# The last 256 output columns of the expert down-projection, made 128 at a time, and the final sums of squares moved from GpSimd to TensorE

## The chip, the cores and the metric

The kernel runs on one core of a Trainium2 chip. The metric is the device time of one execution in microseconds. Of the kernel before there are three timed executions, from 1497.66 to 1500.59 us with a median of 1499.51 us, and one profiled execution of 1500.35 us.

## The reference

The reference computes one layer of a decoder for 288 tokens (256 of a prompt, 8 times 4 of a sample batch) with 2048 channels. The part that matters here is its end: a mixture of 32 experts (gated MLPs with 512 hidden channels each), and after it a gated per-layer embedding and a last normalization. With `h` the residual stream, the end is

```
h = h + sum over the chosen experts e of  weight[e] * (act[e] @ w_down[e])      # 512 -> 2048 for each expert
u = rmsnorm(h, g_ple)                                                             # over the 2048 channels
h = h + sigmoid(u @ w_ple_gate + b_ple_gate) * (p @ w_ple_proj)                   # 2048 -> 2048
y = rmsnorm(h, g_final)
```

`w_down` has 32 x 512 x 2048 fp32 numbers (134 MB), `w_ple_gate` 2048 x 2048 (16.8 MB). Each channel of the second matrix product needs all 2048 channels of `h`, and each norm needs the sum of squares of all of them.

## The kernel before

Everything lies with channels on partitions: `hT` is 16 rows (c = 0 to 15) of 128 channels by 288 tokens. The stage around the change begins when the experts' hidden activations are ready.

The down-projection (the loop that ends the function, L1419 to L1446) runs over 8 blocks of 256 output columns, that is two rows of `hT` each. In a block it runs over 10 units of experts, in the order W N N W N W N W N N: a unit W is two experts with 64 token slots each, a unit N four experts with 32 slots each. A pair of experts is one transfer (L1428) of 128 x 2048 numbers, 1 MB, issued from SyncE's queue into half of a 2 MB slot of the pool `ws1`. There are four slots; a slot is taken again (`wtile`) when the matmuls on its old content are done. For each unit `down` (L1110) makes `Y`, tokens by columns, in PSUM (L1114), and ScalarE and VectorE split it into a high and a low half (`Yh` L1118, `Yl` L1119). One unit later `turn_` (L1410) calls `back`, which multiplies by the unit's 0/1 matrix so that the result stands by channels and tokens (`yp`, L1129, two rows by two matmuls) and adds it to `hT` (L1131, VectorE).

In the same loop the second product is worked off for the rows that are already finished. When block m has begun, the two rows of block m - 1 are final (`final`, L1353) and 16 "gates" are queued, one for each output row c of `z`: `ev_z` (L1403) multiplies the two finished rows by their part of `w_ple_gate` with three matmuls for each row (`mm3`, L229 to L231: high x high, low x high, high x low) and VectorE adds the result to `z` (L1408). `turn_` runs one gate behind a unit W and two behind a unit N. The gate weights come in transfers of 512 KB (`w_pg`, L1371) into `wraw`, which has two buffers. `halves` splits them into `whi` (ScalarE, L225) and `wlo` (VectorE, L226), two buffers each. All these transfers stand in SyncE's queue in program order, so a transfer that waits for a buffer holds up those behind it.

The gates for the last two rows (14 and 15) can't run until the last weights are used. Their weights are loaded at the end by `last_halves` (L1384 to L1400): two transfers into `wraw` (L1392), and one of 1 MB into a weight slot (L1395).

The end (L1519 to L1598) is written out by hand for TensorE, ScalarE and VectorE. `start_z` (L1476) brings a row of `z` into PSUM by a product with the identity, and `gate` adds the six matmuls of rows 14 and 15. VectorE multiplies by the inverse norm (`mul`, L1487), ScalarE takes the sigmoid (L1488), VectorE multiplies by the projected embedding (`f2a`, L1492) and adds to `hT` (`f2b`, L1495), ScalarE squares (`f3`, L1498). The squares are summed over the rows by GpSimd for rows 0 to 11 (`f4p`, L1504 and L1507), and over the channels by TensorE (`f4`, `token_sums` L1464, three matmuls with one column each). `warm(n)` (L1460) is n matmuls whose result nobody reads. Then the inverse root (L253 to L258), `spread` (L290), which brings it to all partitions, the last product (L1596) and the transfers out (L1597).

Of the kernel before, what the change touches and what calls it, by code (L numbers as in the profile page):

```python
# [20 lines left out]
D = 2048  # L21
# [95 lines left out]
def hymba_kernel(ctx, tc, a):  # L117
# [990 lines left out]
    def down(c0, nd, at, sc, ws, wt, two=None):  # L1108
# [7 lines left out]
        if two:  # L1116
            Yh, Yl = (two.tile([128, nd * 128], F32R, name=nm, bufs=2) for nm in ("Yh", "Yl"))
# [222 lines left out]
    last = KD // 2 - 1  # L1340

# [11 lines left out]
    def final(m):  # L1353

        gparts(m)
        for k in range(2):
            c = 2 * m + k
# [8 lines left out]
    def ready(g):  # L1366

        for i in range(max(wg, default=-1) + 1, min(g + 2, 8 * last)):
# [7 lines left out]
    def gate(m, acc, hi, lo, first=True):  # L1376

        gh, gl = gp[m]
        for k in range(2):
            mm3(acc, hi[:, k, :], lo[:, k, :], gh[:, k, :], gl[:, k, :], first and k == 0, k == 1)  # L1380
# [4 lines left out]
    def last_halves(eng=None):  # L1385
# [3 lines left out]
        if i % 2 == 0:  # L1389
            if i < 4:  # L1390
                wr[0] = tl.tile([128, 8, 128], F32, name="wraw", bufs=2)
                dma(wr[0].rearrange("p k c -> p (k c)"), a["w_pg"][28 + i // 2])  # L1392
            elif i == 4:
                t = wtile()[:, 0]
                dma(t.rearrange("p (r a) b -> p r (a b)", r=2), a["w_pg"][30:32].rearrange("r p x -> p r x"))  # L1395
                wr[1] = t.rearrange("p a (k c) -> p (a k) c", c=128)
        src = wr[0][:, 4 * (i % 2):4 * (i % 2) + 4, :] if i < 4 else wr[1][:, 4 * (i % 4):4 * (i % 4) + 4, :]
        hi, lo = (x[:, 4 * (i % 4):4 * (i % 4) + 4, :] for x in pw[i // 4 * 2:i // 4 * 2 + 2])
        nc.scalar.copy(hi, src)
        (eng or nc.vector).tensor_sub(lo, src, hi.bitcast(F32))  # L1400

    def ev_z(m, c):
        acc = psA([128, NTOK], "acc")  # L1403
        gate(m, acc, *[x[:, 2 * (c % 2):2 * (c % 2) + 2, :] for x in ready(8 * m + c // 2)])
# [10 lines left out]

    with tc.manual_schedule(engines={mybir.EngineType.PE}):
        gates += [lambda: None] * 2
        for m in range(KD // 2):
            for u, (s0, ne) in enumerate(units):  # L1419
                wt = []  # L1420
                for i in range(s0 // 2, (s0 + ne) // 2):
                    if not half:
                        t = wtile()
                        half += [t[:, 0], t[:, 1]]
                    t = half.pop(0)
                    src = a["w_down"][m]
                    src = src[0] if i == 0 else src[pair_of(i)].rearrange("o p x -> (o p) x")
                    dma(t, src.rearrange("p (a b) -> p a b", a=4))  # L1428
                    v = t.rearrange("p (e a) (b c) -> p e (a b) c", e=2, c=256)
# [3 lines left out]
                if u == 0 and m:  # L1433
                    final(m - 1)
                    gates += [lambda c=c, m=m: ev_z(m - 1, c) for c in range(KD)]
                back.append(b)
                if m == last:
                    if u == 4:
                        pw.append(ws1.tile([128, 16, 128], F32R, name=pslots[0]))
                    if u == 8:  # L1440
                        t = ws1.tile([128, 2, 16, 128], F32R, name=slots.pop(0)[1])
                        pw += [t[:, 0], None, t[:, 1]]
                        last_halves()
                        last_halves()
# [25 lines left out]
    sqs = tl.tile([128, NTOK], F32, name="sqs")  # L1470
# [29 lines left out]
    def f4p(c):  # L1500

        x = sqt[:, c % 4:c % 4 + 2, :]
        if c == 0:
            nc.gpsimd.tensor_add(sqs, x[:, 0, :], x[:, 1, :])  # L1504
        else:
            for i in range(2):
                nc.gpsimd.tensor_add(sqs, sqs, x[:, i, :])  # L1507

    def f4(c):
        token_sums(pf, sqt[:, c % 4, :], c == 12, c == KD - 1)  # L1510
# [4 lines left out]
    c0 = KD - 2  # L1515
    with tc.manual_schedule(engines={E.PE, E.Activation, E.DVE}):
# [10 lines left out]
        last_halves(nc.gpsimd)  # L1527
        last_halves(nc.gpsimd)
        nc.scalar.activation(gh[:, 0, :], hT[:, c0, :], AF.Copy, scale=prm("g_ple", c0))
        nc.vector.tensor_mul(sqt[:, 0, :], hT[:, c0, :], hT[:, c0, :])  # L1530
        nc.scalar.activation(sqt[:, 1, :], hT[:, c0 + 1, :], AF.Square)
        nc.vector.scalar_tensor_tensor(gl[:, 0, :], hT[:, c0, :], prm("g_ple", c0), gh[:, 0, :].bitcast(F32),
                                       op0=ALU.mult, op1=ALU.subtract)
        split(gh[:, 1, :], gl[:, 1, :], hT[:, c0 + 1, :], prm("g_ple", c0 + 1))
        for c in range(1, 3):
            start_z(c)
        for i in range(2):
            token_sums(ssp, sqt[:, i, :], False, i == 1)
# [6 lines left out]
        last_halves(nc.gpsimd)  # L1545
# [6 lines left out]
        for p in range(KD // 2):  # L1552
# [9 lines left out]
            if nh[0] < 8:  # L1562
                last_halves(nc.gpsimd)
            f0(c + 6)
            f0(c + 7)
            if p > 1:
                if c - 4 < 12:
                    f4p(c - 4)
                else:
                    f4(c - 4)  # L1570
# [119 lines left out]
```

## Time and profile before

| | |
|---|---|
| timed, median of 3 | 1499.51 us (1497.66 to 1500.59) |
| profiled execution | 1500.35 us, span 1498.7 us |
| mean granted TensorE clock | 0.947 |
| TensorE busy | 1300.5 us (87%) |
| VectorE / ScalarE / GpSimd busy | 553.5 / 392.0 / 23.1 us |
| DMA | 518.32 MB, mean 346 GB/s |

The span runs from the first instruction to the last. The profiled execution took 1.65 us more than its span. The down-projection's first weights are used at about 1096 us, its last at 1451 us; what comes after that, to 1498.7 us, is called the tail below.

### The profile page before, as it was taken

To read this page: it belongs to the slowest core of one execution; us is meant where nothing else is said; L and a number is where in the kernel's file an instruction comes from. 1 tells how busy PE (TensorE), PEld (TensorE's weight loads), DVE (VectorE), ACT (ScalarE), POOL (GpSimd) and SP (SyncE) were. 2 spreads that over 40 slices of the span, in tenths; PEclk is the share of its full clock that TensorE was granted. 3 is DMA by queue.
4 is the path that set the end of the run, shared out by engine and by line. 5 is a ranking of instruction groups with operands and counts; after the bars stand their busy time and mean duration, and the time that the engine had idled before them with its cause. 6 is when DMAs were issued, how large, how long until landed. Compare 5 with 4: busy or idle time off the path is not lost.

```text
span 1498.7 us, 24037 instructions
## 1 busy us (share of the span) xinstructions
PE 1300.5 (87%) x9535; PEld 851.1 (57%) x9535; DVE 553.5 (37%) x1322; ACT 392.0 (26%) x744; POOL 23.1 (2%) x26
## 2 busy tenths in 40 slices
PE   7999888799999988775978868869778999999996
PEld 7997677588996444222523423416235666666675
DVE  6765545666663100000000000003023455555557
ACT  6535434655441100000000000002013322222335
POOL 0000000000000000000000000000000000000014
PEclk9999998999999999987999989979899999999997
DMA  7879787532776899999999999999999999999971
GB/s 271 275 242 295 240 277 246 160 141 76 266 273 266 352 396 427 428 427 428 417 428 427 428 428 427 427 426 426 393 418 419 419 419 419 419 419 418 420 287 64
DMA packets 80841, 518.32 MB, mean 346 GB/s; under 512 B 10705, under 2 KB 12818, under 8 KB 47826
## 3 DMA queue, kind: packets, MB, share of 16 engines
q1 hardware_dynamic: 80066, 514.33, 86.3%
q0 software_dynamic: 656, 2.39, 0.4%
q8 instruction: 77, 1.26, 0.3%
q14 instruction: 42, 0.34, 0.1%
HBM read 513.81 MB, written 2.88 MB: 345 GB/s over the span
## 4 chain that ended last, share of the span: by engine, by line
DMA 35%; PE 15%; DVE 2%; issue 1%; ACT 0%; DVEq 0%; SPq 0%; ACTq 0%
DMA w<-in_w_down 21%; DMA w<-in_w_up 8%; PE Gp L1081 6%; DMA w<-in_w_gate 5%; PE xp L1054 4%; PE Y L1114 2%; PE pp L1280 1%; DMA wpp<-in_w_pp 1%; DVE gtt L1492 1%; DVE hT L1495 0%; DVE gtt L1487 0%; DVE hT L1596 0%; PE yp L1129 0%; PE s L1464 0%; PE acc L1460 0%
## 5 line engine op out<-in xcount | busy, mean ns | idle before, releaser
L1081 PE MATMUL Gp<-w,Xq 128*32 128x512 f32 (+1 forms) x2048 | 356.8, 673 | 93.4 <-DMA w<-in_w_up 50.1
L1081 PEld LDWEIGHTS Gp<-w,Xq 128*32 128x32 f32 (+1 forms) x2048 | 89.7, 127 | 318.7 <-issue 175.9
L229 PE MATMUL acc<-uh,whi 128*128 128x288 f32 x496 | 155.6, 314 | 14.9 <-ACT whi L219 7.4
L231 PE MATMUL acc<-uh,wlo 128*128 128x288 f32 x496 | 153.8, 310 | 3.5 <-DVE wlo L220 3.4
L230 PE MATMUL acc<-ul,whi 128*128 128x288 f32 x496 | 152.4, 307 | 0.4 <-DVE ul L264 0.4
L1090 DVE SCALAR_TENSOR_TENSOR Yb<-Gp,rs,Yb 128x512 f32<-128x512 f32 x10 | 7.5, 751 | 341.8 <-PE Gp L1081 307.5
L1131 DVE TENSOR_TENSOR hT<-hT,yp 128x288 f32<-128x288 f32 x160 | 71.2, 450 | 165.2 <-PE yp L1129 165.2
L1054 PE MATMUL xp<-Pq,hn 96*128 96x256 f32 (+1 forms) x576 | 119.8, 360 | 12.8 <-issue 12.0
L1114 PE MATMUL Y<-w,w 128*32 128x256 f32 (+1 forms) x1280 | 113.8, 389 | 19.2 <-DMA w<-in_w_down 19.1
L1054 PEld LDWEIGHTS xp<-Pq,hn 96*128 96x128 f32 x576 | 97.2, 197 | 53.9 <-issue 42.6
L229 PEld LDWEIGHTS acc<-uh,whi 128*128 128x128 f32 x496 | 97.9, 197 | 19.0 <-ACT whi L219 9.2
L220 DVE TENSOR_TENSOR wlo<-wraw,whi 128x1024 fp32r<-128x1024 f32 x82 | 99.9, 1220 | 18.6 <-PE acc L231 9.8
L231 PEld LDWEIGHTS acc<-uh,wlo 128*128 128x128 f32 x496 | 98.0, 198 | 7.4 <-DVE wlo L220 5.8
L219 ACT CAST whi<-wraw 128x1024 fp32r<-128x1024 f32 x82 | 85.4, 1042 | 63.9 <-PE acc L230 45.5
L230 PEld LDWEIGHTS acc<-ul,whi 128*128 128x128 f32 x496 | 98.2, 198 | 1.6 <-DVE ul L264 0.9
L1114 PEld LDWEIGHTS Y<-w,w 128*32 128x32 f32 (+1 forms) x1280 | 51.7, 116 | 66.2 <-DMA w<-in_w_down 34.1
L1058 DVE TENSOR_SCALAR Xq<-xp,P 128x256 f32<-128x256 f32 (+1 forms) x48 | 21.1, 440 | 168.5 <-PE xp L1054 168.5
L1118 ACT ACTIVATE Yh<-Y,wsl 128x256 fp32r<-128x256 f32 x80 | 37.9, 473 | 173.6 <-PE Y L1114 172.9
L1089 ACT ACTIVATE Yb<-Gp,rs 128x512 f32<-128x512 f32 x10 | 6.9, 687 | 283.9 <-PE Gp L1081 278.4
L1114 PE MATMUL Y<-w,wl 128*32 128x256 f32 (+1 forms) x768 | 72.3, 389 | 8.9 <-DMA w<-in_w_down 8.9
L1056 ACT ACTIVATE Xq<-xp,P 128x256 f32<-128x256 f32 (+1 forms) x48 | 21.0, 438 | 189.8 <-PE xp L1054 189.8
L231 PE MATMUL acc<-gh,wlo 128*128 128x288 f32 x224 | 66.1, 295 | 1.3 <-DVE wlo L226 1.3
(487 smaller groups left out, 1868.8 us busy)
## 6 DMA issues: line engine op xcount, KB each, us to landing
w<-in_w_gate SPq DMA_DIRECT2D x64, 2048.0 KB, 26.0
w<-in_w_up SPq DMA_DIRECT2D x64, 2048.0 KB, 24.8
w<-in_w_down SPq DMA_DIRECT2D x128, 1024.0 KB, 17.1
kv<-in_cache SPq DMA_DIRECT2D x128, 288.0 KB, 3.9
wraw<-in_w_in SPq DMA_DIRECT2D x44, 512.0 KB, 4.8
wraw<-in_w_o SPq DMA_DIRECT2D x32, 512.0 KB, 4.0
wraw<-in_w_pg SPq DMA_DIRECT2D x30, 512.0 KB, 15.2
wraw<-in_w_uq SPq DMA_DIRECT2D x6, 512.0 KB, 4.1
```

Of the source, the lines that this page charges most:

```text
L219: nc.scalar.copy(hi[:, x, :], r[:, x, :])
L220: nc.vector.tensor_sub(lo[:, x, :], r[:, x, :], hi[:, x, :].bitcast(F32))
L229: nc.tensor.matmul(out, hi, xh, start=start, stop=False)
L230: nc.tensor.matmul(out, hi, xl, start=False, stop=False)
L231: nc.tensor.matmul(out, lo, xh, start=False, stop=stop)
L1054: nc.tensor.matmul(xp, hn[:, t, d * 128:(d + 1) * 128], Pq[:, t, :n], start=t == 0, stop=t == 2)
L1056: nc.scalar.activation(X[:, d, :n], xp, AF.Copy, scale=prm("g_ffn", d))
L1058: nc.vector.tensor_scalar(X[:, d, :n], xp, prm("g_ffn", d), None, op0=ALU.mult)
L1081: nc.tensor.matmul(acts[j][sl * e:sl * e + sl, :], X[:, kk, o:o + sl], wt[e](k), start=kk == 0, stop=kk == KD - 1)
L1114: nc.tensor.matmul(Y[sl * e:sl * e + sl, :], at[:, f, sl * e:sl * e + sl], w(f), start=f == 0, stop=f == 3)
L1118: nc.scalar.activation(Yh, Y, AF.Copy, scale=ws)
L1131: nc.vector.tensor_add(h_, h_, yp)
```

## The change

The eight blocks of 256 columns become seven of 256 and two of 128. `w_down` is passed as two arrays, `w_down2` with seven blocks and `w_down1` with two; in the last two blocks a pair is a transfer of 512 KB, four to a slot (`wpart`). A block of 128 columns has one row of `hT`, so its `Y` has 128 columns and `back` one `yp` of two matmuls.

When the first of the two narrow blocks is done, row 14 is final. Its 16 gates, of three matmuls each instead of six, are worked off in the last block; `ready` now loads `w_pg` for it too (L1371 becomes L1382). Only row 15 is left for the tail. Its weights, two transfers of 512 KB, are loaded inside the last block by `last_halves` behind units 5 and 7 and split there by ScalarE and VectorE, into a slot taken out of the weights' four at unit 4. In the tail the gate of a row of `z` is three matmuls instead of six, and GpSimd has nothing to do: `f4p` is gone, and `f4` on TensorE sums the squares of all 16 rows. `warm(3)` becomes `warm(2)`.

```diff
+    blocks = [*((2 * m, 2) for m in range(7)), (14, 1), (15, 1)]
+    rows_ = [(2 * m, 2) for m in range(KD // 2 - 1)] + [(KD - 2, 1), (KD - 1, 1)]
+    last = len(rows_) - 1
...
-        for i in range(max(wg, default=-1) + 1, min(g + 2, 8 * last)):
+        for i in range(max(wg, default=-1) + 1, min(g + 2, 60)):
...
     def gate(m, acc, hi, lo, first=True):
         gh, gl = gp[m]
-        for k in range(2):
-            mm3(acc, hi[:, k, :], lo[:, k, :], gh[:, k, :], gl[:, k, :], first and k == 0, k == 1)
+        n = rows_[m][1]
+        for k in range(n):
+            mm3(acc, hi[:, k, :], lo[:, k, :], gh[:, k, :], gl[:, k, :], first and k == 0, k == n - 1)
...
+    def last_halves():
         i = nh[0]
         nh[0] += 1
         if i % 2 == 0:
...
+            wr[1] = tl.tile([128, 8, 128], F32, name="wraw", bufs=2)
+            dma(wr[1].rearrange("p k c -> p (k c)"), a["w_pg"][30 + i // 2])
+        halves(*(x[:, 4 * i:4 * i + 4, :] for x in pw), wr[1][:, 4 * (i % 2):4 * (i % 2) + 4, :])
...
+    def wpart(n):
+        if n == 4:
+            return wtile().rearrange("p e f c -> p (e f c)")
+        if not half or half[0].shape[1] != 1024 * n:
+            t = wtile().rearrange("p e f c -> p (e f c)")
+            half[:] = [t[:, 1024 * n * i:1024 * n * (i + 1)] for i in range(4 // n)]
+        return half.pop(0)
...
-                b = down(2 * m, 2, at[u], sc[u], ws[:, u:u + 1], wt, tl)
-                turn_(ne // 2 + (m == last and u in (6, 8)))
+                b = down(c0, nd, at[u], sc[u], ws[:, u:u + 1], wt, tl)
+                turn_(ne // 2 * max(1, bd // 2))
...
+                if n == len(blocks) - 1:
                     if u == 4:
                         pw.append(ws1.tile([128, 16, 128], F32R, name=pslots[0]))
...
+                        pw.append(ws1.tile([128, 2, 16, 128], F32R, name=slots.pop(0)[1])[:, 0])
+                    if u in (5, 6, 7, 8):
                         last_halves()
...
     def f4(c):
-        token_sums(pf, sqt[:, c % 4, :], c == 12, c == KD - 1)
+        token_sums(pf, sqt[:, c % 4, :], c == 0, c == KD - 1)
...
-                if c - 4 < 12:
-                    f4p(c - 4)
-                else:
-                    f4(c - 4)
-                    f4(c - 3)
+                f4(c - 4)
+                f4(c - 3)
...
-        warm(3)
+        warm(2)
```

Three places show what this moves. The first is SyncE's queue at its end, before: the last transfers of expert weights (`w3_12722`, `w1_12789`), gate weights (`wraw`, `w2_12903`) and the first output. The names in brackets are the semaphores waited for.

```order
L1428 DMA w3_12722<-in_w_down 128x2048 [waits DMAHW3_49,PE_49]
L1428 ISA
L1428 DMA w3_12722<-in_w_down 128x2048 [waits DMAHW4_49]
L1392 DMA wraw_12783<-in_w_pg 128x1024 [waits DMAHW5_49,DVE_49]
L1428 ISA
L1428 DMA w1_12789<-in_w_down 128x2048 [waits DMAHW7_49,DMAHW6_49,PE_49]
L1428 ISA
L1428 DMA w1_12789<-in_w_down 128x2048
L1392 DMA wraw_12853<-in_w_pg 128x1024 [waits DMAHW1_49,DMAHW0_49,DVE_49]
L1395 DMA w2_12903<-in_w_pg 128x2x1024 [waits DMAHW2_49,PE_49]
L1597 DMA out_yT<-hT_4517 128x288 [waits DVE_49,Activation_49]
```

And the same place now (`w4_12967` holds pairs 8 to 11 of the last block, `w1_13065` pairs 12 to 15, which units 8 and 9 use):

```order
L1439 DMA w4_12967<-in_w_down1 128x1024 [waits DMAHW5_49]
L1403 DMA wraw_13061<-in_w_pg 128x1024 [waits DMAHW6_49,DVE_49]
L1439 ISA
L1439 DMA w1_13065<-in_w_down1 128x1024 [waits DMAHW7_49,PE_49]
L1439 ISA
L1439 DMA w1_13065<-in_w_down1 128x1024 [waits DMAHW0_49]
L1439 ISA
L1439 DMA w1_13065<-in_w_down1 128x1024 [waits DMAHW1_49]
L1439 ISA
L1439 DMA w1_13065<-in_w_down1 128x1024 [waits DMAHW2_49]
L1586 DMA out_yT<-hT_4517 128x288 [waits DMAHW3_49,DVE_49,Activation_49]
```

Before, the two transfers that wait for a split of gate weights (DVE_49) at the very end stood behind the last expert weights, and one stood two transfers ahead of them. Now the last one stands four transfers ahead of the end of the expert weights, and nothing of `w_pg` is left behind them.

The second place is VectorE in the last block now, around units 5 and 6: `wlo_13024` is the last split of row 14's gate weights out of the buffer `wraw_12918`, whose memory `wraw_13061` takes over; `w3_12966` are row 15's, out of `wraw_12991`.

```order
L1414 TENSOR_TENSOR z_9330<-z_9330,acc_12955 128x288 [waits PE_49]
L1414 TENSOR_TENSOR z_9330<-z_9330,acc_12960 128x288 [waits PE_49]
L1144 TENSOR_TENSOR hT_4517<-hT_4517,yp_12982 128x288 [waits PE_49]
L1132 SCALAR_TENSOR_TENSOR Yl_12979<-Y_12969,wsl_8884,Yh_12978 128x128 [waits Activation_49]
L1414 TENSOR_TENSOR z_9330<-z_9330,acc_12986 128x288 [waits PE_49]
L226 TENSOR_TENSOR w3_12966<-wraw_12991,wl_12965 128x512 [waits DMAHW2_49,DMAHW1_49,DMAHW4_49,DMAHW0_49,Activation_49]
L226 TENSOR_TENSOR wlo_13024<-wraw_12918,whi_13023 128x512 [waits Activation_49]
L226 TENSOR_TENSOR w3_12966<-wraw_12991,wl_12965 128x512 [waits Activation_49]
```

The split that frees the buffer for the last gate weights (`wlo_13024`) stands behind the sums of row 14's gates up to unit 5's and behind a split of row 15's, which waits for its own transfer.

The third is the end of TensorE's program before, from the gate of the last row of `z` on:

```order
L230 MATMUL acc<-gl,w_12829 128x288
L231 MATMUL acc<-gh,w_12782 128x288
L229 MATMUL acc<-gh,w_12829 128x288
L230 MATMUL acc<-gl,w_12829 128x288
L231 MATMUL acc<-gh,w_12782 128x288
L1460 MATMUL acc<-z,ones 128x288 x5
L1464 MATMUL s_12849<-ones,sqt 96x1 x6
L1464 MATMUL s_12849<-ones,sqs 96x1 x3
L1464 MATMUL s_12849<-ones,sqt 96x1 x6
L1460 MATMUL acc<-z,ones 128x288 x3
L290 MATMUL spread<-diag,ones 128x288
```

and now:

```order
L1486 MATMUL acc<-z,C 128x288
L229 MATMUL acc<-gh,wl 128x288
L230 MATMUL acc<-gl,wl 128x288
L231 MATMUL acc<-gh,w_12966 128x288
L1475 MATMUL s_13161<-ones,sqt 96x1 x24
L1471 MATMUL acc<-z,ones 128x288 x5
L1475 MATMUL s_13161<-ones,sqt 96x1 x12
L1471 MATMUL acc<-z,ones 128x288 x2
L290 MATMUL spread<-diag,ones 128x288
```

The sums over `sqs`, which GpSimd made, are gone, and TensorE has three one-column matmuls for each of the 16 rows (12 more of them stand between the last gates, in two groups of six).

## Rows read from the trace of the kernel before

**Rows 1.** Page, part 2: GB/s moved in each fortieth of the span.

```profile
GB/s 271 275 242 295 240 277 246 160 141 76 266 273 266 352 396 427 428 427 428 417 428 427 428 428 427 427 426 426 393 418 419 419 419 419 419 419 418 420 287 64
```

**Rows 2.** Chain that ended last, last weights: start us, us, what.

```profile
1435.78 13.69 DMA w<-in_w_down
1449.52 1.92 PE Y L1114 x28
1451.44 0.72 PE yp L1129 x4
```

**Rows 3.** SyncE's issues near the end: start us, us, queue, line, what.

```profile
1435.25 0.86 SPq L1428 DMA_DIRECT2D w<-in_w_down  x2
1443.41 0.34 SPq L1392 DMA_DIRECT2D wraw<-in_w_pg  x1
```

**Rows 4.** SyncE's waits, 1080 to 1499 us: total us, times, longest.

```profile
SPq L1392 <- DVE wlo L226: 14.8, 2, 7.6
```

**Rows 5.** DMA issues: KB each, median us from issue to landing.

```profile
wraw<-in_w_o SPq DMA_DIRECT2D x32, 512.0 KB, 4.0
```

**Rows 6.** TensorE, unit 0 of the last block: start us, busy us, instruction.

```profile
1406.69 1.95 PE L1114 MATMUL Y<-w,wl 128*64 128x256 f32 x16
1408.57 0.40 PE L1129 MATMUL yp<-sc,Yh 128*128 128x288 f32 x1
...
1409.20 0.30 PE L229 MATMUL acc<-gh,whi 128*128 128x288 f32 x1
...
1409.86 0.29 PE L231 MATMUL acc<-gh,wlo 128*128 128x288 f32 x1
1410.08 0.63 PE L1114 MATMUL Y<-w,wl 128*32 128x256 f32 x4
```

**Rows 7.** TensorE in the attention: 32-column weights with 256 and with 128 columns moved.

```profile
207.79 1.05 PE L503 MATMUL Ss<-kv,qls 128*32 128x256 f32 x16
208.65 0.62 PE L507 MATMUL Ss<-kv,qrs 128*32 128x128 f32 x16
```

**Rows 8.** TensorE after two microseconds without work, early in the down-projection.

```profile
1124.84 3.61 PE L1114 MATMUL Y<-w,w 128*32 128x256 f32 x28 [1.72 <-DMA w<-in_w_down]
```

**Rows 9.** VectorE, one split of half a weight buffer: start us, busy us.

```profile
1447.34 0.69 DVE L1400 TENSOR_TENSOR w<-wraw,wl 128x512 fp32r<-128x512 f32 x1
```

**Rows 10.** VectorE's groups, 1459 to 1483 us: busy us, mean ns, idle before.

```profile
L1492 DVE TENSOR_TENSOR gtt<-gtt,proj 128x576 f32<-128x576 f32 x7 | 8.0, 1148 | 0.3 <-ACT gtt L1488 0.3
L1495 DVE TENSOR_TENSOR hT<-hT,gtt 128x576 f32<-128x576 f32 x7 | 7.3, 1047 | 0.0
L1487 DVE TENSOR_TENSOR gtt<-acc,acc 128x288 f32<-128x288 f32 x16 | 7.0, 447 | 1.5 <-ACT acc L1546 1.5
```

**Rows 11.** ScalarE's groups, 1459 to 1483 us: busy us, mean ns, idle before.

```profile
L1488 ACT ACTIVATE gtt<-gtt,P 128x288 f32<-128x288 f32 x16 | 8.4, 533 | 4.7 <-DVE gtt L1487 4.6
L1498 ACT ACTIVATE sqt<-hT 128x576 f32<-128x576 f32 x7 | 4.7, 672 | 0.5 <-DVE hT L1495 0.5
L1513 ACT ACTIVATE hT<-hT,P 128x288 f32<-128x288 f32 x6 | 2.9, 522 | 0.0
```

**Rows 12.** GpSimd's sums of squares, 1451 to 1499 us: busy us, mean ns.

```profile
L1507 POOL TENSOR_TENSOR sqs<-sqs,sqt 128x288 f32<-128x288 f32 x10 | 11.4, 1141 | 2.3 <-ACT sqt L1498 1.6
```

**Rows 13.** Chain that ended last, in the tail: start us, us, what.

```profile
1461.10 0.76 DVE gtt L1492
...
1482.64 0.45 ACT sqt L1498
1483.13 1.97 PE s L1464 x12
1485.11 3.09 PE acc L1460 x6
1488.20 0.97 PE spread L290 x2
1489.19 0.82 DVE hT L1596 x2
```

**Rows 14.** Busy us and instructions of each engine, granted clock, DMA share, GB/s.

```profile
core 0: us, PE busy (x) PEld busy (x) DVE busy (x) ACT busy (x) POOL busy (x), PEclk, DMA share, GB/s
1400.00:1420.00 20.00, 19.09 (x182) 13.35 (x181) 12.45 (x30) 7.37 (x14) 0.00 (x0) 1.00 1.02 420
1460.00:1480.00 20.00, 18.50 (x112) 16.36 (x110) 19.70 (x30) 15.63 (x31) 14.71 (x14) 1.00 0.00 1
1480.00:1499.00 19.00, 7.71 (x38) 5.94 (x38) 9.64 (x20) 7.51 (x16) 1.78 (x2) 0.59 0.33 125
```

More of the change, by code (lines that the diff above doesn't have):

```diff
@@ L1023, in oload, with wdown @@
         return [lambda k, e=e: one(e, k) for e in range(2)]
+    blocks = [*((2 * m, 2) for m in range(7)), (14, 1), (15, 1)]
+    rows_ = [(2 * m, 2) for m in range(KD // 2 - 1)] + [(KD - 2, 1), (KD - 1, 1)]
+    last = len(rows_) - 1
+    def wdown(b):
+        nd = blocks[b][1]
+        return a[f"w_down{nd}"][b - next(i for i, x in enumerate(blocks) if x[1] == nd)]
     def olast(n, i, e):
@@ L1355, in final @@
         gparts(m)
-        for k in range(2):
-            c = 2 * m + k
+        for k in range(rows_[m][1]):
+            c = rows_[m][0] + k
             split(gp[m][0][:, k, :], gp[m][1][:, k, :], hT[:, c, :], prm("g_ple", c))
@@ L1389, in last_halves @@
         if i % 2 == 0:
[L1390 to L1400, printed above, removed]
+            wr[1] = tl.tile([128, 8, 128], F32, name="wraw", bufs=2)
+            dma(wr[1].rearrange("p k c -> p (k c)"), a["w_pg"][30 + i // 2])
+        halves(*(x[:, 4 * i:4 * i + 4, :] for x in pw), wr[1][:, 4 * (i % 2):4 * (i % 2) + 4, :])
     def ev_z(m, c):
         acc = psA([128, NTOK], "acc")
-        gate(m, acc, *[x[:, 2 * (c % 2):2 * (c % 2) + 2, :] for x in ready(8 * m + c // 2)])
+        n = rows_[m][1]
+        i, o = divmod(n * c, 4)
+        gate(m, acc, *[x[:, o:o + n, :] for x in ready(8 * m + i)])
         if m == 0:
@@ L1414, in turn_ @@
             gates.pop(0)()
+    def wpart(n):
[5 more added lines that the diff above has]
+        return half.pop(0)
     with tc.manual_schedule(engines={mybir.EngineType.PE}):
-        gates += [lambda: None] * 2
-        for m in range(KD // 2):
+        for n, (c0, nd) in enumerate(blocks):
+            b0, bd = blocks[n - 1] if n else (0, 0)
             for u, (s0, ne) in enumerate(units):
@@ L1430, in hymba_kernel @@
-                    wt += [lambda f, e=e, v=v: v[:, e, f, :] for e in range(2)]
-                b = down(2 * m, 2, at[u], sc[u], ws[:, u:u + 1], wt, tl)
-                turn_(ne // 2 + (m == last and u in (6, 8)))
-                if u == 0 and m:
-                    final(m - 1)
-                    gates += [lambda c=c, m=m: ev_z(m - 1, c) for c in range(KD)]
+                    w = wdown(n)
+                    t = wpart(nd)
+                    dma(t, w[0] if i == 0 else w[pair_of(i)].rearrange("o p x -> (o p) x"))
@@ new lines, in hymba_kernel @@
+                    v = t.rearrange("p (e f c) -> p e f c", e=2, f=4)
+                    wt += [lambda f, e=e, v=v: v[:, e, f, :] for e in range(2)]
+                b = down(c0, nd, at[u], sc[u], ws[:, u:u + 1], wt, tl)
+                turn_(ne // 2 * max(1, bd // 2))
+                if u == 0 and n:
+                    while gates:
+                        gates.pop(0)()
+                    for m, (r0_, rn) in enumerate(rows_):
+                        if b0 <= r0_ < b0 + bd:
+                            final(m)
+                            gates += [lambda c=c, m=m: ev_z(m, c) for c in range(KD)]
```

61 lines of the change are left out of this document (16 added, 45 removed).

## The prediction

> **What bounds the kernel now.** I read the bandwidth by slices first, then the chain of waits from its end backwards, then SyncE's queue, and last the busy times of the tail. From slice 30 on the weights come at 419 GB/s without a break [rows 1], and the chain there is one weight transfer behind the other: the last one is issued at 1435.78 and lands at 1449.47, the last unit's `Y` then has 28 of its 32 matmuls left, and `yp` starts at 1451.44 [rows 2]. TensorE is busy 19.09 of 20 us in this stage [rows 14], so it trails the transfers closely: whatever makes either later shows in the time. From 1451.44 on nothing is loaded. In the tail VectorE is busy 19.70 of 20 us, ScalarE 15.63, GpSimd 14.71 and TensorE 18.50 [rows 14], with VectorE on the chain; after 1482.64 a serial end follows, square, token sums, three `warm`, `spread`, output [rows 13], at a mean clock of 0.59 [rows 14].
>
> So there are two stages to price: how late the last `yp` comes, and how long the rest takes from there.
>
> **The narrow blocks on TensorE.** A unit W takes 3.39 us: `Y` 1.88, four `yp` 0.63, six gate matmuls and the way back to `Y` 0.88, with 0.132 a matmul (five steps from 1409.20 to 1409.86) [rows 6]. A unit N runs twelve gate matmuls, 0.79 more: 4.18. With half the columns, sixteen matmuls in four sets of four took 0.62 instead of 1.05 [rows 7], 0.108 a set less; `Y` has eight sets, so it falls by 0.86 to 1.02, and two `yp` go, 0.27. In the first narrow block the gates are those of two rows as before: W 2.26, N 3.05, and four W and six N make 27.3. That is for half the columns, where a wide block takes 4 x 3.39 + 6 x 4.18 = 38.6: gates and hand-overs don't shrink. In the second narrow block the gates are those of one row: W 1.86, N 2.26, with the first unit still at 2.26.
>
> The first narrow block starts where the last wide one did, at 1406.69 [rows 6]. Up to the gate of unit 5 the second takes 2.26 + 3 x 2.26 + 2 x 1.86 - 0.22 (the step from the last gate matmul to the next `Y`) = 12.5, up to the `yp` behind the last `Y` 2.26 + 5 x 2.26 + 3 x 1.86 + 1.02 = 20.2. If TensorE never waited, that `yp` would start at 1406.69 + 27.3 + 20.2 = 1454.2, 2.8 later than before.
>
> **The queue.** It will wait. The last gate weights (`wraw_13061`) are in SyncE's queue ahead of the four last expert transfers, and their buffer is free only after the split `wlo_13024`; this needs the `whi` and `wlo` that gates 4 to 7 of row 14 use, and gate 7 is unit 5's. Before, the wait at this place was also long (two waits, 14.8 us together [rows 4]), but only gate weights stood behind the second: it was issued at 1443.41, when the last expert weights had been issued at 1435.25 [rows 3]. Now gate 7 ends at 1406.69 + 27.3 + 12.5 + 0.3 = 1446.8. ScalarE's cast and VectorE's subtraction take about 0.7 each (the latter 0.69 [rows 9]), with 0.2 for hand-overs: 1448.4. Everything else that is loaded by then is 1 MB less than what had landed before at 1449.47 (2 MB of experts less, two gate transfers more), or 2.5 us at 419 GB/s: the transfers run dry near 1447 to 1448, just when the queue reopens. A transfer of 512 KB into an idle queue landed 4.0 after its issue [rows 5]: 1452.4. The four behind it follow at 0.52 MB / 419 GB/s = 1.25: 1457.4. Then some 0.9 of the last `Y` remain, and after a wait of some 4 us the clock is low: after a shorter one 28 matmuls of `Y` took 3.61 [rows 8] instead of 1.92 [rows 2]. For less work at half size I take 0.5, between 0 and 1.7. The `yp` starts at 1458.8, **7.4 late**. From both sides: 2.8 if the queue costs nothing, and 11 if the transfer restarts two microseconds slower than into an idle queue, and the full 1.7 is paid.
>
> Of the 4 KB rows that the narrow transfers have (8 KB before) the trace shows no price in this stage; the stages with 2 MB transfers moved 427 GB/s against 419 here [rows 1], so smaller pieces may cost 2%, or 0.8 us of the last 40, none of it seen by an end that waits for the queue.
>
> **The tail.** Two `yp` matmuls (0.27) and six of the twelve token sums go ahead of the loop; two columns' sums, twelve matmuls, take 1.97 at the low clock [rows 13], so six at the full one some 0.5: -0.8.
>
> In the loop GpSimd's sums go (11.4 us [rows 12]) and its splits of weights. Beside it VectorE's `gtt` and `hT` products of 576 columns took 1.148 and 1.047 on average [rows 10]; the first, with GpSimd still, took 0.76 [rows 13]. If all fourteen take 0.76, that is 15.3 - 10.6 = 4.7 less. A pair of rows on VectorE is then 2 x 0.76 + 2 x 0.447 = 2.41. ScalarE has for a pair two sigmoids, a square and, for three pairs, two scalings: 2 x 0.533 + 0.672 + 2 x 0.522 = 2.78 [rows 11]. In these three it falls behind by 0.37 each: 1.1. TensorE loses three gate matmuls in each of 16 rows, 48 x 0.132 = 6.3, and gains 36 token sums, some 3 to 6 us: it stays as full as it was. I take -3.5 for the loop, between 0 (TensorE's sums set the pace) and -4.7.
>
> In the Trainium skill, "SBUF — State Buffer", section "Who interferes with whom", VectorE and GpSimd are said to share a port pair that one instruction holds to its end. The rows above agree for the products with two SBUF inputs (0.76 against 1.148), and by the rule alone the loop would gain the whole 4.7.
>
> At the end three `warm` become two: 3.09 / 3 [rows 13], -1.0; `spread` waits for them, since its input was ready before. Bounds: -0.5 at the full clock, -1.5 if the clock rises too. Together -0.8 - 3.5 - 1.0 = **-5.3**, between -1.3 and -7.
>
> **The sum.** +7.4 - 5.3 = +2.1 on the profiled execution of 1500.35, whose span is 1.65 shorter: 1502.45. That execution lies 0.84 above the median of the runs, so 1501.6 is what I forecast. A measurement of this kernel can tell about 0.2%, 3.0 us, from no change: the forecast is a loss inside that.
>
> **Rivals.**
> The queue costs nothing (16%): TensorE decides and its `yp` is 2.8 late. For it: the transfers run dry only when the queue reopens, within the two microseconds by which my sum of TensorE's units may be off, and a transfer that meets others still on their way need not pay the whole 4.0. Against: four transfers behind a 4.0 us landing can't be hidden by anything still queued. 2.8 - 5.3 = -2.5: 1497.0.
>
> The tail gives little (18%): the token sums set TensorE's pace in the loop, and waits pull its clock to the low level early, as the 0.59 of the last stretch shows that it can. The point from which this decides is where a pair's sums (1.97 at the low clock) with its gates exceed VectorE's 2.41. Then only 0.8 and 1.0 are gained: +7.4 - 1.8 = +5.6, 1505.1.
>
> The last weights land as before and the tail gains in full (12%): the other side. The bytes are the same, and if TensorE is quicker than I add up, gate 7 comes before 1443 and the queue never runs dry. Against: this needs 4 us of 40 from rows that agree to 0.1. 0 - 5.3: 1494.2, faster.
>
> Small transfers lose rate (4%): the 32 narrow transfers run at three quarters of the rate, 314 instead of 419 GB/s, and 16.8 MB take 53.4 instead of 40.0. With the slack between the blocks +12, and 1500.35 + 12 - 5.3 - 0.84: about 1506.5 or more. Against it: the gate weights are pieces of 512 KB already, and the stage with them holds 419 [rows 1].
> In the Trainium skill, "DMA: Bandwidth & Descriptors", section "Bandwidth", the rule is to make transfers of at least 1 MiB for three quarters of the peak, which speaks against halving them; the trace has no stretch of such transfers alone that would show it in a full queue.
>
> **How the numbers follow.** The forecast has 50%, with its own range 1498.5 to 1504.7; of this 31 lie within 0.2% of the median and 19 above. Of the first rival's 16, 7 are faster and 9 the same; of the second's 18, 2 the same and 16 slower; the third's 12 are faster, the last's 4 slower. Faster 0.19, same 0.42, slower 0.39. The range reaches down to 1496.0, which leaves out most of the third rival and a little of the first, and up to 1506.5, which leaves out the far end of the second and the last.
>
> **What would show it.** Right: on SyncE a wait of L1403 for `wlo` that ends between 1447 and 1450, with the last four L1439 behind it; a gap in the transfers there; TensorE idle for about 4 us ahead of unit 8; `yp` behind the last `Y` at 1457 to 1461; narrow units of 2.3 and 3.05 us; VectorE's products at about 0.75 throughout. Wrong: transfers without a gap to 1455, VectorE's products at 1 us without GpSimd, or a loop in which VectorE waits for TensorE's `acc`.

## The result and the profile after

The changed kernel takes 1507.0 us (median of 5, 1506.73 to 1509.61) against 1499.51 before: 1.0055 times as long, 95% interval 1.0043 to 1.0067. Forecast were 1501.6, within 1496.0 to 1506.5, and a loss that can hardly be told. The profiled execution took 1506.73, with a span of 1505.1 against 1498.7. Of these 6.4 us, the last `yp` accounts for 8.9 (it starts at 1460.27 instead of 1451.37), and the tail from there to the end gives back 2.5 (44.8 instead of 47.3). The narrow blocks began 0.9 earlier than the wide one before (1405.80 instead of 1406.69), so the stage of the last weights itself is 9.8 longer.

**The weights.** SyncE's last issues, and its wait ahead of the last gate weights (in total, times, longest):

```profile
1437.83 0.34 SPq L1403 DMA_DIRECT2D wraw<-in_w_pg  x1
1438.36 1.38 SPq L1439 DMA_DIRECT2D w<-in_w_down  x3
1448.40 0.34 SPq L1403 DMA_DIRECT2D wraw<-in_w_pg  x1
1448.99 1.92 SPq L1439 DMA_DIRECT2D w<-in_w_down  x4
```
```profile
SPq L1403 <- DVE wlo L226: 8.6, 1, 8.6
```

This answers to [rows 3, 4]: between 1439.74 and 1448.40 SyncE issues nothing. The gate transfer goes out at 1448.40, the very time forecast, and the last four expert transfers behind it. TensorE then (start, busy, what ended the idle time before):

```profile
1453.28 0.41 PE L1127 MATMUL Y<-w,w 128*32 128x128 f32 x4 [2.06 <-DVE w L226]
1455.51 1.24 PE L1127 MATMUL Y<-w,w 128*32 128x128 f32 x28 [1.82 <-DMA w<-in_w_down]
1458.90 1.43 PE L1127 MATMUL Y<-w,w 128*32 128x128 f32 x32
1460.27 0.40 PE L1142 MATMUL yp<-sc,Yh 128*128 128x288 f32 x1
```

Two waits of some 2 us for unit 8's two transfers, and then nearly all of units 8 and 9 is still to do. The first wait is put down to a split of row 15's gate weights, which unit 8's `Y` doesn't read; the transfer that it does read, issued at 1448.99, landed 4.2 later, at 1453.2. The other three landed at 1455.5, 1457.0 and 1458.2. A narrow unit N itself took what was forecast, 1408.34 to 1411.43, 3.09 (forecast 3.05), and its `Y` 1.01:

```profile
1408.34 1.08 PE L1127 MATMUL Y<-w,wl 128*32 128x128 f32 x32
1409.35 0.40 PE L1142 MATMUL yp<-sc,Yh 128*128 128x288 f32 x1
...
1411.43 0.43 PE L1127 MATMUL Y<-w,wl 128*32 128x128 f32 x8
```

**The tail.** Before, the marks from which it is counted were these: the last `yp`, TensorE's five `warm` (ten instructions) with the pause behind them, and the last square:

```profile
1451.37 0.40 PE L1129 MATMUL yp<-sc,Yh 128*128 128x288 f32 x1
...
1475.91 2.59 PE L1460 MATMUL acc<-z,ones 128*128 128x288 f32 x10
1481.09 1.18 PE L1464 MATMUL s<-ones,sqt 128*96 128x1 f32 x12 [2.59 <-ACT sqt L1498]
```
```profile
1483.30 0.44 ACT L1498 ACTIVATE sqt<-hT 128x288 f32<-128x288 f32 x1 [0.21 <-issue]
```

Now VectorE's two products, which answer to [rows 10], and the chain at the end, which answers to [rows 13]:

```profile
L1502 DVE TENSOR_TENSOR gtt<-gtt,proj 128x576 f32<-128x576 f32 x7 | 5.3, 753 | 1.8 <-ACT gtt L1498 1.8
L1505 DVE TENSOR_TENSOR hT<-hT,gtt 128x576 f32<-128x576 f32 x7 | 5.2, 747 | 0.0
```
```profile
1481.29 5.39 PE s L1475 x48
1486.68 4.44 PE acc L1471 x10
1491.12 1.97 PE s L1475 x24
...
1494.83 0.77 PE spread L290 x2
1495.62 2.81 DVE hT L1585 x5
```

The products fell from 1.148 and 1.047 to 0.75 each. From `yp` to the first `mul` (1467.70) it is 7.43 instead of 8.24, from there to the start of the last square (1486.77, within the row "1486.42 0.79" below) 19.1 instead of 23.7 (1459.61 to 1483.30). But from the last square to the last product it is 8.85 instead of 5.9: when ScalarE starts that square, TensorE has just come out of 48 instructions of token sums, then runs the five `warm` (ten instructions) at 4.44, and only then the last sums. Its busy time and granted clock by stretches of the tail, with the DMA stage ahead:

```profile
1420.00:1440.00 20.00, 20.00 (x288) 17.36 (x287) 14.80 (x35) 8.17 (x17) 0.00 (x0) 1.00 1.03 410
1440.00:1460.00 20.00, 15.88 (x215) 12.73 (x217) 12.47 (x31) 5.40 (x12) 0.00 (x0) 0.91 0.71 263
1480.00:1485.00 5.00, 5.00 (x48) 4.89 (x46) 3.76 (x7) 3.54 (x8) 0.00 (x0) 0.86 0.00 0
1485.00:1490.00 5.00, 5.00 (x18) 4.04 (x18) 1.67 (x5) 3.06 (x6) 0.00 (x0) 0.50 0.00 0
```
```profile
1486.42 0.79 ACT L1508 ACTIVATE sqt<-hT 128x288 f32<-128x288 f32 x2 [0.42 <-DVE hT L1505]
```

TensorE is never idle in the profile from 1480 to 1490, and still the granted clock falls to 0.50, the lower level of 1.2 GHz, behind the one-column sums.

The late sums hold the loop too. `sqt` has room for the squares of four rows, so a new square waits until TensorE has summed an old one. Two of ScalarE's squares waited for that, 0.42 and 1.27; behind each stand sigmoids on ScalarE, and VectorE waited 0.65 for them both times. The longer wait, and VectorE's behind it:

```profile
1482.26 0.68 ACT L1508 ACTIVATE sqt<-hT 128x576 f32<-128x576 f32 x1 [1.27 <-PE s L1475]
```
```profile
1483.40 0.76 DVE L1502 TENSOR_TENSOR gtt<-gtt,proj 128x576 f32<-128x576 f32 x1 [0.65 <-ACT gtt L1498]
```

### The profile page after: what moved, and what is told of

Read it like the earlier page. It is cut to its first block, busy times and chain, and to the rows that moved or that the text cites. A ratio compares the mean times of both kernels' runs of the same rounds, so it can differ in the third digit from the quotient of the medians.

```text
span 1505.1 us, 24737 instructions
## 1 busy us (share of the span) xinstructions
PE 1307.2 (87%) x9849; PEld 862.9 (57%) x9849; DVE 560.5 (37%) x1355; ACT 394.2 (26%) x754; POOL 3.0 (0%) x9
## 4 chain that ended last, share of the span: by engine, by line
DMA 32%; PE 19%; DVE 1%; issue 1%; ACT 0%; SPq 0%; DVEq 0%; ACTq 0%
DMA w<-in_w_down 19%; DMA w<-in_w_up 8%; PE Gp L1094 6%; DMA w<-in_w_gate 4%; PE xp L1067 4%; PE Y L1127 3%; PE pp L1293 1%; PE yp L1142 1%; PE s L1475 1%; PE acc L231 1%; PE acc L230 1%; PE acc L229 1%; PE acc L1486 0%; DVE hT L1585 0%; PE acc L1471 0%
## 5 line engine op out<-in xcount | busy, mean ns | idle before, releaser
L1127 PE MATMUL Y<-w,w 128*32 128x256 f32 (+2 forms) x1440 | 113.2, 365 | 23.7 <-DMA w<-in_w_down 21.4
L1127 PEld LDWEIGHTS Y<-w,w 128*32 128x32 f32 (+1 forms) x1440 | 55.5, 116 | 67.0 <-DMA w<-in_w_down 34.7
L1131 ACT ACTIVATE Yh<-Y,wsl 128x256 fp32r<-128x256 f32 (+1 forms) x90 | 40.5, 450 | 188.4 <-PE Y L1127 187.9
L1127 PE MATMUL Y<-w,wl 128*32 128x256 f32 (+3 forms) x864 | 72.0, 360 | 7.5 <-DMA w<-in_w_down 7.5
L231 PE MATMUL acc<-gh,wlo 128*128 128x288 f32 x240 | 71.1, 296 | 1.4 <-DVE wlo L226 1.4
L230 PE MATMUL acc<-gl,whi 128*128 128x288 f32 x240 | 71.2, 297 | 0.0
```

The lines of the kernel that those rows point to most:

```text
L230: nc.tensor.matmul(out, hi, xl, start=False, stop=False)
L231: nc.tensor.matmul(out, lo, xh, start=False, stop=stop)
L1127: nc.tensor.matmul(Y[sl * e:sl * e + sl, :], at[:, f, sl * e:sl * e + sl], w(f), start=f == 0, stop=f == 3)
```

## The experiments

The theory: two losses that have nothing to do with each other. SyncE's held queue delays the last weights, and the narrow blocks alone cost some; and in the tail TensorE's queue of token sums and `warm` matmuls, at the low clock, takes back most of what VectorE gains. Against it stand: the transfers of half the size cost by themselves; the bytes, not the order, decide; idle GpSimd is worth nothing; the `warm` matmuls are needed for the clock.

The stage of the expert weights began between 1092.5 and 1099.1 us in the profiled executions (1095.2 in that of the kernel before), so single profiles are compared from the start of the block that begins at about 1406 (the last wide one before, the first narrow one after). "Weights" is from there to the `yp` behind the last `Y`, "tail" from that to the end of the span.

| kernel | weights | tail | time, median | ratio to before, 95% |
|---|---|---|---|---|
| before | 44.7 | 47.3 | 1499.51 | |
| after | 54.5 | 44.8 | 1507.0 | 1.0043 to 1.0067 |
| e1_own_buffers | 49.2 | 43.5 | 1502.73 | 1.0011 to 1.0029 |
| e1_pg_last | 48.6 | 46.3 | 1503.21 | 1.0014 to 1.0035 |
| e2_no_warm5 | 54.4 | 42.2 | 1503.76 | 1.0022 to 1.0043 |
| e3_gpsimd_sums | 56.3 | 43.0 | 1506.89 | 1.0033 to 1.0058 |
| e4_own_nowarm | 49.7 | 42.7 | 1500.6 | 0.9992 to 1.0013 |
| e5_before_te_sums | 45.2 | 49.3 | 1502.25 | 1.0005 to 1.0025 |
| e7_own_gpsimd | 49.7 | 42.9 | 1501.73 | 0.9996 to 1.0020 |
| e8_own_ones | 49.8 | 41.8 | 1499.42 | 0.9988 to 1.0008 |
| e9_before_ones | 44.3 | 47.7 | 1499.54 | 0.9993 to 1.0011 |
| e10_narrow_late | 48.0 | 42.8 | 1498.23 | 0.9981 to 0.9999 |
| e11_two_products | 50.1 | 44.8 | 1501.65 (one run) | |

Each ratio is to executions of the kernel before made beside that version (medians 1499.51 to 1499.91). "Weights" and "tail" come from one profiled execution each, so differences of a few tenths between versions aren't told apart.

**The held queue: e1_own_buffers.**

```diff
-            wr[1] = tl.tile([128, 8, 128], F32, name="wraw", bufs=2)
-            dma(wr[1].rearrange("p k c -> p (k c)"), a["w_pg"][30 + i // 2])
+            x = (sqt, gtt)[i // 2].rearrange("p k c -> p (k c)")[:, :1024]
+            dma(x, a["w_pg"][30 + i // 2])
+            wr[1] = x.rearrange("p (k c) -> p k c", c=128)
```

> The changed kernel, with the last two gate-weight transfers landing in memory of their own (that of sqt and gtt, free until the tail), so that they wait for no split and SyncE is not held in front of the last four expert transfers. Theory (the blocked queue): the transfers run on without a gap, TensorE's own pace decides, yp behind the last Y starts at 1454 to 1455.5 instead of 1460.34 and the time falls by 5 to 6.5, to about 1501. Rival (the smaller transfers are the cost, by their rate or their latency): yp moves by less than 2 and the time stays above 1505.

SyncE's last issues and TensorE's last unit:

```profile
1440.15 0.34 SPq L1406 DMA_DIRECT2D gtt<-in_w_pg  x1
1441.52 4.08 SPq L1443 DMA_DIRECT2D w<-in_w_down  x4
```
```profile
1455.18 1.30 PE L1127 MATMUL Y<-w,w 128*32 128x128 f32 x32
1456.41 0.40 PE L1142 MATMUL yp<-sc,Yh 128*128 128x288 f32 x1
```

The last four go out from 1441.52, 7.5 earlier, and the weights stage is 5.3 shorter, the time 4.3 (5.2 by the two ratios). That is the held queue, though not the whole of what I expected (`yp` at 1456.4 in an execution whose block began 1.4 later than the changed kernel's, and 1502.7 instead of 1501).

**Order against bytes: e1_pg_last.**

```diff
-                    if u in (5, 6, 7, 8):
+                    for _ in range((5, 6, 9, 9).count(u)):
                         last_halves()
```

> The changed kernel, with the last gate-weight transfer (w_pg 31) issued behind the last expert transfer instead of four ahead of it; its wait stays. Theory (the blocked queue): yp behind the last Y at 1454 to 1455, time 1500.5 to 1501.5, and the late gate weights are in time for rows 8 to 15 of z. Rival (bytes, not order): the same transfers have to land, only another is last; the tail then waits for the gate weights, and the time stays above 1504.

The weights stage is 48.6, 5.9 shorter, so the order decides. But the tail is 1.5 longer than the changed kernel's: VectorE splits the late gate weights between the last `Yl` and the last row's addition, and this stands on the chain:

```profile
1456.38 1.29 DVE w L226 x2
1457.67 0.36 DVE z L1414
1458.04 0.38 DVE hT L1144
```

The time is some 2 above what I expected, below the rival's 1504.

**The five warm matmuls: e2_no_warm5** (`warm(5)` deleted).

> The changed kernel without the five warm matmuls between the token sums of rows 4 to 11 and those of rows 12 to 15. Theory (TensorE's queue at the low clock ends the tail): the last sums end 4 to 4.5 earlier, 1502.5. Rival (the warm matmuls hold the clock, and the sums would run into the low clock earlier): the sums and the spread get longer by what goes, 1506 or more.

The tail is 2.6 shorter, the time 3.2. TensorE's end is now:

```profile
1480.00 3.14 PE L1475 MATMUL s<-ones,sqt 128*96 128x1 f32 x36
1483.30 1.18 PE L1475 MATMUL s<-ones,sqt 128*96 128x1 f32 x12 [0.16 <-ACT sqt L1508]
1484.92 3.83 PE L1475 MATMUL s<-ones,sqt 128*96 128x1 f32 x24 [0.44 <-ACT sqt L1508]
1488.61 2.27 PE L1471 MATMUL acc<-z,ones 128*128 128x288 f32 x4
```
```profile
1485.00:1487.00 2.00, 2.00 (x14) 2.00 (x15) 0.55 (x2) 1.69 (x3) 0.00 (x0) 0.54 0.00 0
```

It waits for ScalarE again, as it should. Of the 4.4 that the `warm` rows took, 1.9 were lost again, since the last 24 sums take 3.83 instead of 1.97: that is the low clock, granted 0.54 and then 0.50 here, where those of the changed kernel, behind its `warm`, ran at 1.00 from 1491 on. Both readings were right in part, the theory's for the larger one.

**The sums back on GpSimd: e3_gpsimd_sums, and e7_own_gpsimd with the queue free.** As the kernel before: `f4p` for rows 0 to 11, into `z[:, 1, :]`.

> The changed kernel with the sums of squares of rows 0 to 11 back on GpSimd (into memory of a row of z that is no longer read), the rest as changed: narrow blocks, three-matmul gates, warm(2). Theory: VectorE's products fall back from 0.75 to 1.0 to 1.1 us and its loop gets 3 to 4 longer, TensorE's end gets 4 shorter: 1506 to 1508. Rival one (the sums on TensorE alone spoil the tail): 1503 or less. Rival two (idle GpSimd is worth its full gain): 1510 or more.

> The changed kernel with the last gate weights in memory of their own and the sums of rows 0 to 11 on GpSimd. Theory (the sums belong to GpSimd as long as TensorE sums them three columns at a time): the tail of the GpSimd kernel, 42.9 from the last yp, behind a yp at 1456 to 1457: span 1499, as long as before (1498.7) or 1 above. Rival (idle GpSimd pays once the queue is free): 2 or more above the same kernel with sums on TensorE (1499.9), so 1502.

In e3 the loop takes 20.6 instead of 19.1, with products of 0.92 and 0.88 on average, the end from the last square 5.3 instead of 8.85, and the tail is 1.8 shorter than the changed kernel's. The time is that of the changed kernel within the intervals, as the theory had it, so neither rival's time came. The profiled execution itself is 2.0 longer: its narrow blocks began 2.0 later, and its weights took 1.8 more. The gain of the tail thus stands in the profile and isn't shown by the times. In its tail the five `warm` cost nothing: they ran at the full clock, and TensorE waited behind them.

```profile
1484.82 2.69 PE L1471 MATMUL acc<-z,ones 128*128 128x288 f32 x10
1490.33 1.18 PE L1475 MATMUL s<-ones,sqt 128*96 128x1 f32 x12 [2.82 <-ACT sqt L1509]
```

With the queue free (e7) the tail is again 42.9 and the time 1501.73. The rival asked for a longer time than with the sums on TensorE (1502.73, e1_own_buffers) and fell; the theory had the time at most 1 above the kernel before, where the medians say 1.8, with an interval from 0.6 below to 3 above. So moving the sums to TensorE in this form was a loss of 0.6 to 1.8 in the tail of the profiles (43.5 against 42.9, 44.8 against 43.0), which the times alone don't show clear of their intervals. The rest of the change there, three-matmul gates, no splits on GpSimd, one row and one `warm` less, gives 4.3 (e3 against before).

**The sums alone on the kernel before: e5_before_te_sums.**

```diff
-                if c - 4 < 12:
-                    f4p(c - 4)
-                else:
-                    f4(c - 4)
-                    f4(c - 3)
+                f4(c - 4)
+                f4(c - 3)
```

> The kernel before with one part of the change: TensorE makes the sums of squares of all 16 rows, GpSimd only splits the last gate weights; wide blocks, six-matmul gates, five and three warm matmuls stay. Theory (TensorE's queue sets the end of the tail once the sums are on it): VectorE's loop gets up to 3 shorter, but sums and warm matmuls run on at the low clock behind it: 2 to 6 slower than before, 1502 to 1506. Rival (the sums alone are a gain, as VectorE gets its port): 1 to 3 faster, 1497 to 1499.

2.3 slower; the tail is 2.0 longer (49.3 instead of 47.3). VectorE's products are shorter (0.855 and 0.957), but now it waits, as [rows 10] had not shown:

```profile
L1492 DVE TENSOR_TENSOR gtt<-gtt,proj 128x576 f32<-128x576 f32 x7 | 6.0, 855 | 4.6 <-ACT gtt L1488 4.6
```

Its loop is 24.3 (1460.01 to 1484.30) against 23.7: with six-matmul gates TensorE sets the pace. Three of ScalarE's squares wait 4.8 in all for TensorE's sums to free `sqt`, and VectorE's 4.6 stand behind them. So taking the sums off GpSimd shortens the loop only together with the halved gates: 24.3 by itself, 20.6 with the gates halved and the sums on GpSimd (e3), 19.1 with both.

**Both cures: e4_own_nowarm** (e1_own_buffers without `warm(5)`).

> Both cures together: the last gate weights in memory of their own, and no five warm matmuls. Theory (two separate losses, the held queue of 4 to 6 us and TensorE's end of 2.5 to 4): the gains add up, span 1496.5 to 1498, time 1 to 2 below the kernel before. Rival (they overlap: with the weights earlier the tail waits elsewhere): not better than the first cure alone, span 1499.5 or more.

The parts add up, in the profile (49.7 and 42.7, together 0.4 longer than before) and in the time (the ratio is 1.0003 against 1.0020 of e1_own_buffers, 2.5 us better, where `warm(5)` was worth 2.6 in the tail of e2). But the time isn't below the kernel before, where I expected it 1 to 2 below. The span of 1495.9 is as short as that only because this execution's narrow blocks began 3.2 earlier than the wide one before.

**Another form of the sums: e8_own_ones, and e9_before_ones on the kernel before.**

```diff
     def f4(c):
-        token_sums(pf, sqt[:, c % 4, :], c == 0, c == KD - 1)
+        if c == 0:
+            pf.append(psB([128, NTOK], "acc"))
+        nc.tensor.matmul(pf[0], ones, sqt[:, c % 4, :], start=c == 0, stop=c == KD - 1)
```

> The changed kernel with the last gate weights in memory of their own, and the sums on TensorE in another form: one product of an all-ones matrix with the 288 columns of squares for each row (two instructions where the token sums have six), summed up in PSUM, so that every partition holds the sum and no spread and no warm matmul is left; the inverse root is then taken of 288 columns. Theory (it is the form of the sums that keeps TensorE behind, not that TensorE makes them): the first sum after the last square ends within 1 us, the inverse root takes some 3, and the span is 1494 to 1497. Rival (TensorE is behind since its gates are): the end comes no sooner than without the warm matmuls, 1497 or more.

> The kernel before, wide blocks and six-matmul gates, with the sums of squares on TensorE in the all-ones form (one product of 288 columns a row, no spread, no warm matmuls); GpSimd only splits the last gate weights. Theory (narrow blocks cost 4 to 5 even with a free queue, and the tail's gain comes from taking the sums off GpSimd in a form that TensorE can keep up with): last yp as before at 1451 to 1452, loop 3 shorter, end 0 to 1 shorter, span 1494 to 1497, time 1495.5 to 1498, faster than both kernels. Rival (with six-matmul gates TensorE is already full in the loop, so sums in any form slow it, as the token sums did): span 1499 to 1501.

In e8 the last sums take 2.2 where the token sums of e2 took 3.8, and no `spread` is left, but the reciprocal is now one of 288 columns:

```profile
1484.72 2.21 PE L1517 MATMUL acc<-sqt,ones 128*128 128x288 f32 x8 [0.39 <-ACT sqt L1510]
```
```profile
1487.93 1.95 DVE L1586 RECIPROCAL gtt<-gtt 128x288 f32<-128x288 f32 x1 [0.51 <-ACT gtt L1585]
```
```profile
1484.00:1486.00 2.00, 1.61 (x7) 1.05 (x6) 1.34 (x4) 1.58 (x4) 0.00 (x0) 1.00 0.00 0
```

The fewer instructions aren't the gain: at the full clock the token sums of four rows took 1.97 (after), and six rows take 3.14 in either form (e2, e8). It is the clock, which stays at 1.00 to the end here without any `warm`.

The tail is the shortest of all, 41.8, by 0.9 to that without `warm`; the span of this profile (1500.8) missed what I expected, in part because its narrow blocks began 2.5 later than the wide one before. The time is that of the kernel before. On the kernel before itself (e9) the form gains nothing, as the rival said: the chain there runs through TensorE's gates, one row of `z` each 1.28 us:

```profile
1465.46 0.48 PE acc L1476 x2
1466.74 0.48 PE acc L1476 x2
```

**What holds the narrow blocks once the queue is free: e11_two_products and e10_narrow_late.**

```diff
+            if m in (6, 7):
+                nc.tensor.matmul(acc, hi[:, k, :], gh[:, k, :], start=first and k == 0, stop=False)
+                nc.tensor.matmul(acc, lo[:, k, :], gh[:, k, :], start=False, stop=k == n - 1)
+                continue
             mm3(acc, hi[:, k, :], lo[:, k, :], gh[:, k, :], gl[:, k, :], first and k == 0, k == n - 1)
```

> The kernel with the gate weights in memory of their own, and the gates of rows 12 to 14, which run inside the narrow blocks, with two of their three products (high x low left out): TensorE has 6.3 us less to do there, the transfers are the same. From the start of the first narrow block to the last yp it was 49.2 to 49.9. Theory (TensorE at 47.5 and the transfers, which end at 46.5, both hold it): 47.5 to 48.3. Rival one (TensorE alone): 43 to 45. Rival two (the transfers alone): 49 to 50.

50.1: rival two. With 6.3 us less to do, TensorE only waits more, busy 9.15 of 12 us, while the transfers run at their full share almost to 1452 (columns as in [rows 14]):

```profile
1440.00:1452.00 12.00, 9.15 (x132) 6.90 (x136) 8.51 (x22) 4.04 (x9) 0.00 (x0) 1.00 1.01 401
```

In e10 both transfers of row 15's gate weights go behind the last expert transfer, as they did before; ScalarE and GpSimd split them in the tail, and the sums have the all-ones form.

```diff
-                    if u in (5, 6, 7, 8):
-                        last_halves()
+                    if u == 9:
+                        for i in range(2):
+                            raw.append(tl.tile([128, 8, 128], F32, name="wraw", bufs=2))
+                            dma(raw[i].rearrange("p k c -> p (k c)"), a["w_pg"][30 + i])
```

> Narrow blocks with both of row 15's gate-weight transfers behind the last expert transfer, split by ScalarE and GpSimd in the tail, and sums in the all-ones form. Theory (two things hold the narrow blocks' end: 1 MB of gate weights ahead of the last expert weights, 2.5 us, and TensorE's own 47.5 from the first narrow block's start): yp comes 48 after that start instead of 49.2 to 49.9, tail 42, time 1497 to 1499. Rival (the order of the transfers is without effect once nothing waits): 49 to 50, and 1499.5 or more.

48.0, tail 42.8, time 1498.23, ratio 0.9990 (0.9981 to 0.9999): as the theory said, and the only version whose interval lies below the kernel before, by 0.1% and hardly (its upper end is 0.9999, and one of eleven versions may do that by chance). The stages of its profile add up to 90.8 for 92.0 before. In the narrow blocks TensorE now waits for nothing:

```profile
1420.00:1440.00 20.00, 20.00 (x288) 17.23 (x287) 14.79 (x35) 8.17 (x17) 0.00 (x0) 1.00 1.03 410
1440.00:1452.00 12.00, 12.00 (x182) 9.93 (x181) 8.73 (x23) 3.02 (x8) 0.00 (x0) 1.00 1.03 407
```

So 48.0 is TensorE's own time for the two narrow blocks, 3.3 above what the wide one took; 1.2 to 1.8 more (49.2 to 49.8) go once the 1 MB of gate weights isn't loaded ahead of the last expert weights, and 5 to 6 more come from SyncE being held. The rates of the full queue, 407 to 410 GB/s against 419 to 420 before, show the small transfers' price: 2 to 3%, which e10 hides.

The queue isn't free everywhere in these versions, though. At the start of the narrow blocks SyncE is held a first time by the same kind of wait, the longest one of e1_own_buffers:

```profile
SPq L1382 <- DVE wlo L226: 13.4, 3, 7.3
```
```profile
1410.00:1420.00 10.00, 10.00 (x153) 8.74 (x143) 8.02 (x20) 3.88 (x10) 0.00 (x0) 1.00 0.82 299
```

Before, the wait at this place took 6.4, and the transfers went on at 420 GB/s [rows 14], for three transfers of 1 MB had been issued ahead of it. Now these three have 512 KB each, and the queue runs dry: 299 GB/s for 10 us, 1.1 MB less than at 410. TensorE isn't idle there, and in e10, where the same wait is 7.2 long, nothing comes of it. But where the transfers hold the end, as in e1_own_buffers, they run with this arrear; which part of the 1.2 to 1.8 it is, no run shows.

## Why the prediction was wrong

- **The wait on SyncE** was right in place and cause, and taking it away moved the weights by 5.3 to 5.9. That it ended at 1448.40 for 1448.4 is luck: the narrow blocks began 0.9 earlier than I had them, and it ended 0.9 later from there. Gate 7 came 0.5 late, and the split then took 0.4 more than I had counted, as it stood behind a split of row 15's on VectorE. The first wait, at the start of the narrow blocks, I had not seen.
- **The narrow blocks on TensorE** were right: 47.5 summed from the rows, 48.0 where nothing else holds them (e10). A loss of 3 in any case, because gates and hand-overs aren't halved with the columns.
- **The last `yp`** came 8.9 late for 7.4, within the bounds of 2.8 to 11; from the start of the narrow blocks it is 9.8, so 2.4 were missing. Besides the 0.9 of the wait, the last transfer landed 9.8 after the queue reopened, at 1458.2, where I had 9.0: the gate transfer took 3.4 for 4.0, but the four behind it followed at 1.2 to 2.3 each instead of 1.25. And I had let only the last `Y` remain behind them, 0.9 and 0.5. In truth unit 8 was left too when its second transfer came at 1455.5, in part at the low clock, so that unit 9 waited for none, and `yp` came 2.1 behind the last landing for 1.4.
- **VectorE's products and the loop** were right in size: 0.75, and 4.6 less for 3.5 (bounds 0 to 4.7). The fourteen products gave 4.8 for the 4.7 that I had summed; what I had left out is that the two single `gtt` products at the end, 2.0 beside GpSimd, take 0.8. VectorE waited 1.5 more for ScalarE's sigmoids (1.8 after 0.3), where I had 1.1, but that these agree is luck: I had ScalarE fall behind by its own work, and 1.3 of it came of squares that waited for TensorE's sums.
- **The end of the tail** is the step that failed. I wrote "three `warm` become two: ... -1.0", and of TensorE in the loop that "it stays as full as it was". As a sum of busy time that held roughly; as an order it didn't. In program order 24 of the 36 added sums stand behind the last gate, where before no sums of rows 4 to 11 stood. `warm(5)`, in a pause of TensorE before (2.59 and then 2.59 idle) and in e3, came to stand between them and the last sums, at the low clock. The end got 2.95 longer instead of 1.0 shorter, and with it the tail gained 2.5 for 5.3. Without `warm(5)` 2.6 of it come back (e2). I had this as the rival "the tail gives little", but with its price in the loop, where only those 1.3 arose, and with the end still 1.0 shorter.
- The two errors, 2.4 and 2.8, have the same sign. Less the 0.9 by which the narrow blocks began earlier in this execution they add to 4.3, of the 5.4 between forecast and time; the rest is the 0.84 that I took off, since the profiled execution before lay that much above its median, while this one lies 0.3 below its own.
- The rule that VectorE and GpSimd share a port pair ("SBUF — State Buffer" of the Trainium skill, "Who interferes with whom") agrees with these rows: products of 0.75 with GpSimd idle, 1.148 and 1.047 beside it. But by e5 that gain is worth nothing where TensorE sets the pace.
- The rival of small transfers, beside which the prediction had named the rule of at least 1 MiB for three quarters of the peak ("DMA: Bandwidth & Descriptors" of the Trainium skill, "Bandwidth"), fell: 407 to 410 GB/s in a full queue of 512 KB transfers, far from the 314 that I had priced. Its time, "about 1506.5 or more" (the sum as it stands there gives 1506.2), is near the 1507.0 measured, for another reason.

## What to carry to other kernels

When work moves to an engine that has time in sum, write down where in its program order the new instructions will stand and what they wait for: whatever is cheap filling in a pause stands in the way once the pause is gone. A transfer that waits for a buffer must not be put ahead of transfers that the end needs, and even without a wait it delays them by its bytes. Halving the transfers also halves what is queued ahead of such a wait. Halving a tile halves only what scales with it; here the gates and hand-overs made two narrow blocks 3.3 us longer than the wide one.

## What the runs showed of the hardware

- The clock fell to the lower level with TensorE busy for 5.00 of 5 us (1485 to 1490, granted 0.50), behind 48 instructions of one-column products. In e8, with products of 288 columns in their place and TensorE busy for 1.61 of 2 us (1484 to 1486), it stayed at 1.00. Busy time in the profile is no promise of the clock.
- A reciprocal of 128 x 288 on VectorE took 1.95 us, where that of 96 x 3 took 0.17 and the simple operations of 288 columns beside it 0.46 (e8).
- 512 KB transfers in a full queue moved 407 to 410 GB/s (e10), 1 MB ones with gate weights of 512 KB between them 419 to 420 (before).
